# Summing four of seven pairs of modulation vectors by accumulating DMAs instead of matmuls with ones

## The chip, the cores and the metric

The kernel runs on one core of one Trainium2 chip. The metric is the time of the whole program on the device, in microseconds (us); the time before is 1242.71 us, the median of three runs (1241.77 to 1243.41). The engines are TensorE (PE; PEld is its weight load), VectorE (DVE), ScalarE (ACT), GpSimd (POOL) and SyncE (SP), which here only issues DMAs. Each runs its own instructions in a fixed order and waits on semaphores. POOL issues a few DMAs too, those that add to their destination among them.

## The reference

Two layers over 256 latent tokens of width 1024, with 256 context tokens beside them in the first layer. Each layer is a half-step feed-forward block, a mixer (neighbourhood attention in layer 0, a short convolution in layer 1) and a second feed-forward block. Each of these scales, shifts and gates its tokens by modulation vectors, which come from a conditioning vector through a large matrix:

```
for i in range(DEPTH):
    m = (s_c @ ada_w[i] + ada_b[i]).reshape(B, N_MOD, 1, D)     # 9 vectors of 1024 per layer
    mc = (s_cc @ ada_w[i] + ada_b[i]).reshape(N_MOD, D)         # the context's own
    x = half_step_ffn(x, m[:, 0], m[:, 1], m[:, 2], ...)        # shift, scale, gate
    ...
    hx = modulate(x, m[:, 3], m[:, 4])                          # mixer, gate m[:, 5]
    ...
    x = half_step_ffn(x, m[:, 6], m[:, 7], m[:, 8], ...)
```

`ada_w[i]` has 1024 x 9216 float32 entries, so the modulation vectors alone load some 75 MB. What follows is about how these vectors are summed.

## The kernel before, in words

All arithmetic is float32-like: a matrix is split into a high and a low part on ACT (high) and DVE (low), and a product takes three matmuls. PE's order is the program's. The other engines' instructions are placed by a scheduler that works with priorities, so their order can move when anything in the program moves; SP's DMAs too stand in one fixed order, and a DMA that waits holds back all that stand behind it.

The first feed-forward block runs on latent and context tokens together (`f0_mm`, the matmuls at L730, and `out_gemm`). Beside it, in the background, `stream` computes modulation vectors in seven groups of two; a "tick" after each few matmuls moves it on. For one group, `ada` loads 128 x 1024 blocks of `ada_w` (tile `ar`, L317), multiplies each by 128 values of the conditioning vector, one per partition, and adds it to an accumulator of 128 x 1024 on DVE (`acc`, L306 and L308). There are two buffers for accumulators. What is left is a sum over the 128 partitions: four matmuls with a tile of ones (L343), 512 columns each, which write to a PSUM bank; DVE adds the bias (L344), and two DMAs on SP put the vectors into a table in DRAM, `scr` (L346). Groups are counted from 0; groups 0 to 2 are the gates, shifts and scales that are needed first (vectors 2, 3 and 4 of layer 0 for both token sets), group 3 is vectors 5 and 6 of layer 0, group 4 is 7 and 8, groups 5 and 6 are vectors 0 to 3 of layer 1. Later vectors are made in another way on POOL (`sum_up`), with an add-accumulating DMA of 4 KB into `scr` (L358).

The vectors are read from `scr` as rows that are broadcast over partitions (`gate`, L378) or as columns (`mrow` at L394, in `fold_cols`).

Then comes attention. In each of 16 steps a pair of heads gets its scores (L1052 on PE); DVE adds a bias to them (L1056). A bias tile is loaded by SP with small DMAs from a table (L933) and gets a mask added on POOL (L937). There are four bias tiles, so the load of a bias waits until the scores two pairs earlier have been read. Between the steps the projections of keys, values and queries run as a filler, and at the end the output projection (`wo`).

Of the kernel before, what the change touches and what calls it, by code (L numbers as in the profile page):

```python
# [10 lines left out]
F32 = mybir.dt.float32  # L11
# [3 lines left out]
ALU = mybir.AluOpType  # L15
# [3 lines left out]
P = 128  # L19
D = 1024  # L20
# [39 lines left out]
ROPE_EARLY = 70  # L60
S_EARLY = 40
V_LAG = 1
AHEAD = 3
P_EARLY = 70
V_EARLY = 70
# [11 lines left out]
def backbone_kernel(  # L77
# [6 lines left out]
    nc = tc.nc  # L84
    sync = nc.sync
# [16 lines left out]
    def nm(s):  # L102
        uid[0] += 1
        return f"{s}_{uid[0]}"
# [10 lines left out]
    def tpb(s="tp"):  # L115
        return bank("tp", s)
# [125 lines left out]
    win_sb = cp.tile([P, 64], F32, tag="wmask", name="wmask")  # L242
# [4 lines left out]
    lnc = cp.tile([P, 2], F32, tag="lnc", name="lnc")  # L247
# [29 lines left out]
    scr = [tc.dram_tile([2, 9 * D], F32, name=f"scr{i}") for i in range(2)]  # L277
# [10 lines left out]
    def ada(vecs):  # L288


        acc = {}

        def accumulate(l, m, k, w):
            with ExitStack() as st:
                for i in gate_ins + (last_lo if on_pool[0] else []):
                    st.enter_context(tc.issue_after(i.ins))
                for i, vec in enumerate(vecs):
                    if vec[:2] != (l, m):
                        continue
                    if k == 0:  # L300
                        acc[i] = hp.tile([P, D], F32, tag="acc", bufs=2, name=nm("acc"))
                    sc = cst[:, k, vec[2]:vec[2] + 1]
                    for h in range(2):
                        src, a = (c[:, h * 512:(h + 1) * 512] for c in (w, acc[i]))
                        if k == 0:
                            nc.vector.tensor_scalar(a, src, sc, None, op0=ALU.mult)  # L306
                        else:
                            nc.vector.scalar_tensor_tensor(out=a, in0=src, scalar=sc, in1=a,  # L308
                                                           op0=ALU.mult, op1=ALU.add)
            if on_pool[0] and k == KC - 1:  # L310
                sums.extend((vec, acc[i]) for i, vec in enumerate(vecs) if vec[:2] == (l, m))

        loaded = []
        for l, m in dict.fromkeys((l, m) for l, m, _ in vecs):
            for k in range(KC):
                w = hp.tile([P, D], F32, tag="ar", bufs=3, name=nm("ar"))
                sync.dma_start(w, ada_w[l, k * P:(k + 1) * P, m * D:(m + 1) * D])  # L317
                loaded.append((l, m, k, w))
                if len(loaded) > (ADA_LAG if gate_ins else 0):
                    accumulate(*loaded.pop(0))  # L320
                yield 1
        while loaded:
            accumulate(*loaded.pop(0))
            if loaded:
                yield 1
        if on_pool[0]:
            return
        n = 2 * len(vecs)
        if not bias_rows:
            bias_rows.append(hp.tile([P, 512], F32, tag="adab", name=nm("adab")))  # L330
            nc.gpsimd.memset(bias_rows[0], 0.0)
        bt = bias_rows[0]
        for i, (l, m, v) in enumerate(vecs):
            sync.dma_start(bt[64 * i:64 * i + 64:32], ada_b[l, m * D:(m + 1) * D].rearrange("(a b) -> a b", b=512))
        yield 1
        yield 1
        yield 1
        rows = hp.tile([P, 512], F32, tag="adar", name=nm("adar"))
        ps = tpb("ada")
        for i in range(len(vecs)):  # L340
            for h in range(2):
                j = 2 * i + h
                nc.tensor.matmul(ps[32 * j:32 * j + 32, :], ones, acc[i][:, h * 512:(h + 1) * 512], start=True, stop=True)  # L343
        nc.vector.tensor_tensor(out=rows[:32 * n], in0=ps[:32 * n], in1=bt[:32 * n], op=ALU.add)  # L344
        for i, (l, m, v) in enumerate(vecs):
            sync.dma_start(scr[l][v, m * D:(m + 1) * D].rearrange("(a b) -> a b", b=512),  # L346
                           rows[64 * i:64 * i + 64:32, :])
        yield 1

    def sum_up():  # L350
        mark = [nc.gpsimd.tensor_tensor(out=warm, in0=g[0:1, 0:1], in1=lnc[0:1, 0:1], op=ALU.add)
# [10 lines left out]
    made = [0]  # L362
# [46 lines left out]
    def queued(ins):  # L409

        es = ExitStack()
        for i in ins:
            es.enter_context(tc.issue_after(i.ins))
        return es
# [17 lines left out]
    def finish_stats(st):  # L432
        mv = sm.tile([P, 2], F32, tag="mv", bufs=6, name=nm("mv"))
        norm_ins[:] = [nc.vector.bn_aggr(mv, st)]
        rs = sm.tile([P, 1], F32, tag="rs", bufs=6, name=nm("rs"))
        nc.gpsimd.tensor_tensor(out=rs, in0=mv[:, 1:2], in1=lnc[:, 0:1], op=ALU.add)
        nc.gpsimd.tensor_tensor(out=rs, in0=rs, in1=lnc[:, 1:2], op=ALU.pow)
        return mv, rs

    fence = []  # L440
    norm_ins = []
    first_mv = []

# [58 lines left out]
    def run(gen):  # L502
        for _ in gen:
            pass
# [247 lines left out]
    for q, (k0, n) in enumerate(steps):  # L752
        nxt = start_step(*steps[q + 1]) if q < 4 else iter(())
        for g in range(6 * n):
            for _ in range(NS[min(q, 2)][g]):
                next(nxt, 0)
            k = k0 + g // 6
            if k < KC - 1:
                z, part = ZP[g % 6]
                for j in range(3):  # L760
                    f0_part(b0[j][z], 0, u0, j, z, k, part)
            else:
                f0_mm(b0[g % 6 // 2][g % 2], 0, u0, g % 6 // 2, g % 2, (k,))
        run(nxt)
    sync.dma_start(win_sb, win_mask)
    sync.dma_start(rope, rope_tab.rearrange("(t p) a b -> p t a b", p=P))
    w_early[0] = W_EARLY
# [156 lines left out]
    def bias_pair(h, qt, last=False):  # L924


        for hh in (h, h + 1):
            if last:
                bt = rtile(256).rearrange("p (a b) -> p a b", a=4)
            else:  # L930
                bt = hp.tile([P, 4, 64], F32, tag="bias", bufs=4, name=nm("bias"))
            for i in range(2):
                bias_dma[:] = [sync.dma_start(bt[64 * i:64 * i + 64],  # L933
                                              bass.AP(na_rpb_rev.tensor,
                                                      na_rpb_rev.offset + hh * 465 + (7 - 2 * qt - i) * 31 - 48,
                                                      [[1, 64], [31, 4], [1, 64]]))]
            nc.gpsimd.tensor_tensor(out=bt, in0=bt, in1=win_sb[:, ::-1].unsqueeze(1).to_broadcast([P, 4, 64]),  # L937
                                    op=ALU.add)
            BIAS[hh, qt] = bt[:, :, ::-1]

    w_qkv = na_w_qkv[0]
# [94 lines left out]
        res.append(Late(2, rest))  # L1036

    oT = []
    bias_dma = []
    KV, Q = [], []  # L1040

    def scores(h, qt):
# [99 lines left out]
    fill_some(A_PRE + 1)  # L1142
    for i in range(len(steps) + LAG + V_LAG):
        if i == NX_AT:
            new_x(0, 0, s2t)
            for t in range(2):
                for h in range(2):
                    sync.dma_start(xscr[t * P:(t + 1) * P, h * 512:(h + 1) * 512], xt[t][h])
        while i + AHEAD < len(steps) and len(KV) <= steps[i + AHEAD][0] // 4:
            fill_some(1)  # L1150
        if i < len(steps) and i % 2 == 0:
            with tc.high_priority(offset=S_EARLY):
                prs[i], prs[i + 1] = scores(*steps[i])
            for j in range(i + 2 if i <= BIAS_AT else i + 4, i + (3 if i < BIAS_AT else 5), 2):
                if i % 2 == 0 and j < len(steps):
                    bias_pair(*steps[j], j > BIAS_AT + 2)
        credit += rate[min(i, len(rate) - 1)]
        n = int(credit)
        credit -= n
        if i >= V_LAST and fin is None:  # L1160
            run(fill)
            fin = last_filler()
            fill = islice(fin, 10)
        fill_some((n + 1) // 2)
        if i == len(steps) + LAG - 1:
            run(fill)
        if 0 <= i - LAG < len(steps):
            with tc.high_priority(offset=P_EARLY):
                probs_T(*steps[i - LAG], prs.pop(i - LAG))
        fill_some(n // 2)  # L1170
        j = i - LAG - V_LAG
        if j >= 0 and steps[j][1] == 1:
            with tc.high_priority(offset=V_EARLY):
                values(steps[j][0])
    run(fill)
    run(islice(fin, 1))

    def first_unit(u, *behind):
# [8 lines left out]
    phase = tc.tile_pool(name="ph2", bufs=1)  # L1187
    hp = phase.__enter__()
    on_pool[0] = True
    sync.dma_start(scr[1][0, 4 * D:9 * D].rearrange("(a b) -> a b", a=16), ada_b[1, 4 * D:9 * D].rearrange("(a b) -> a b", a=16))  # L1190
    ext[0] = 2

    v0 = made[0]
# [128 lines left out]
```

## Time and profile before

| | |
|---|---|
| median of three runs | 1242.71 us |
| the profiled execution | 1243.97 us, of it the span from first to last instruction 1242.2 us |
| PE busy | 1224.0 us, 99% of the span |
| DVE, ACT, POOL busy | 77%, 52%, 7% |
| chain that ended last | PE 89%, DVE 4%, DMA 2%, ACT 2% |
| first feed-forward block | until about 385 us |
| attention | about 385 to 595 us |

Busy times are shares of the span, and a busy PE is not PE at its peak. The chain that ended last is followed back from the last instruction, at each step to what released it. The view of stretches gives for each engine its busy time in a piece of the span with the number of its instructions, the granted clock of TensorE as a share of full speed, the busy share of the 16 DMA engines and what they moved.

### The profile page before, as it was taken

The numbers are of one execution on the slowest core, as the hardware profiler recorded it, in microseconds if no ns is written. First come the engines' busy times: TensorE is split into PE (matmuls) and PEld (weight loads), VectorE is DVE, ScalarE is ACT, GpSimd is POOL, SyncE is SP. The second block draws the span as 40 slices with busy tenths as digits, with TensorE's granted clock in tenths as the row PEclk, the third lists the DMA queues.
The fourth block names the chain that finished last, engine by engine and source line by source line (L and its number), as shares of the span: only waits on it lengthen the run. The fifth ranks groups of instructions, "written<-read, shape, count | busy, mean of one in ns | idle before, by whom it ended". The sixth has DMA issues, their size and how long they took to land.

```text
span 1242.2 us, 17397 instructions
## 1 busy us (share of the span) xinstructions
PE 1224.0 (99%) x5878; PEld 999.2 (80%) x5878; DVE 962.5 (77%) x1675; ACT 646.6 (52%) x1233; POOL 81.7 (7%) x93
## 2 busy tenths in 40 slices
PE   8999999999999999999999999999999999999997
PEld 5787778778778878887888888888888877888886
DVE  3598997778868767889877677878868798777646
ACT  2433132321325566678787635678635745677531
POOL 0000000000001111120000020020200100000100
PEclk9999999999999999999999999999999999999999
DMA  9976578778852654563899857899776664899741
GB/s 298 303 248 231 183 239 293 260 254 281 296 180 68 177 119 96 125 149 108 258 315 287 278 202 251 231 284 319 228 253 217 212 221 153 231 289 275 245 155 67
DMA packets 232241, 275.69 MB, mean 222 GB/s; under 512 B 59558, under 2 KB 178846, under 8 KB 232152
## 3 DMA queue, kind: packets, MB, share of 16 engines
q1 hardware_dynamic: 231956, 274.54, 71.9%
q8 instruction: 46, 0.75, 0.2%
q14 instruction: 43, 0.35, 0.1%
q0 software_dynamic: 160, 0.02, 0.0%
q10 hardware_dynamic: 36, 0.02, 0.0%
HBM read 265.27 MB, written 2.20 MB: 215 GB/s over the span
## 4 chain that ended last, share of the span: by engine, by line
PE 89%; DVE 4%; DMA 2%; ACT 2%; issue 1%; SPq 1%; POOL 0%; DVEq 0%; ACTq 0%
PE f L730 19%; PE w L171 17%; PE w L172 17%; PE w L174 17%; PE wkv L171 2%; PE wkv L172 2%; PE wkv L174 2%; PE wc L171 1%; PE wc L174 1%; PE wc L172 1%; DMA ar<-in_ada_w_dram 1%; PE S L1052 1%; PE hT L455 1%; PE PT L1077 1%; DVE wcl L220 1%
## 5 line engine op out<-in xcount | busy, mean ns | idle before, releaser
L220 DVE TENSOR_TENSOR w1l<-w1r,w1h 128x512 fp32r<-128x512 f32 (+1 forms) x352 | 226.9, 689 | 45.0 <-ACT w1h L217 44.0
L217 ACT ACTIVATE w1h<-w1r 128x512 fp32r<-128x512 f32 (+1 forms) x352 | 198.7, 618 | 116.8 <-DMA w1r<-in_ffn_w_in_dram 46.1
L171 PE MATMUL w<-w1h,hTh 128*128 128x512 f32 x528 | 206.3, 391 | 1.2 <-ACT hTh L119 1.2
L172 PE MATMUL w<-w1l,hTh 128*128 128x512 f32 x528 | 205.5, 389 | 0.0
L308 DVE SCALAR_TENSOR_TENSOR acc<-ar,cst,acc 128x512 f32<-128x512 f32 x266 | 189.3, 759 | 10.3 <-DMA ar<-in_ada_w_dram 10.2
L171 PE MATMUL w<-w2h,gh 128*128 128x512 f32 (+1 forms) x446 | 173.4, 389 | 0.0
L172 PE MATMUL w<-w2l,gh 128*128 128x512 f32 (+1 forms) x446 | 172.2, 387 | 0.0
L217 ACT ACTIVATE w2h<-w2r 128x512 fp32r<-128x512 f32 x176 | 101.5, 624 | 135.4 <-PE w L174 119.4
L220 DVE TENSOR_TENSOR w2l<-w2r,w2h 128x512 fp32r<-128x512 f32 x176 | 118.3, 713 | 59.1 <-ACT w2h L217 57.2
L174 PE MATMUL w<-w1h,hTl 128*128 128x512 f32 x528 | 162.6, 389 | 0.0
L174 PE MATMUL w<-w2h,gl 128*128 128x512 f32 (+1 forms) x446 | 136.1, 386 | 0.0
L730 PE MATMUL f<-h0h,w1h 128*128 128x512 f32 x352 | 132.4, 392 | 1.9 <-ACT w1h L217 1.5
L730 PE MATMUL f<-h0l,w1h 128*128 128x512 f32 x352 | 133.1, 391 | 0.0
L730 PE MATMUL f<-h0h,w1l 128*128 128x512 f32 x352 | 132.8, 390 | 0.0
L171 PEld LDWEIGHTS w<-w1h,hTh 128*128 128x128 f32 x528 | 99.1, 188 | 22.6 <-ACT hTh L119 2.1
L174 PEld LDWEIGHTS w<-w1h,hTl 128*128 128x128 f32 x528 | 99.0, 188 | 20.9 <-DVE hTl L120 0.4
L172 PEld LDWEIGHTS w<-w1l,hTh 128*128 128x128 f32 x528 | 99.2, 188 | 20.5 <-DVE w1l L220 0.2
L171 PEld LDWEIGHTS w<-w2h,gh 128*128 128x128 f32 x446 | 83.8, 188 | 19.2 <-issue 1.7
L172 PEld LDWEIGHTS w<-w2l,gh 128*128 128x128 f32 x446 | 83.8, 188 | 17.0 <-DVE w2l L220 0.5
L174 PEld LDWEIGHTS w<-w2h,gl 128*128 128x128 f32 x446 | 83.3, 188 | 17.1
L730 PEld LDWEIGHTS f<-h0h,w1h 128*128 128x128 f32 x352 | 65.7, 188 | 19.6 <-issue 3.4
L730 PEld LDWEIGHTS f<-h0l,w1h 128*128 128x128 f32 x352 | 65.6, 188 | 14.3 <-issue 0.8
(216 smaller groups left out, 1783.1 us busy)
## 6 DMA issues: line engine op xcount, KB each, us to landing
w1r<-in_ffn_w_in_dram SPq DMA_DIRECT2D x340, 256.0 KB
ar<-in_ada_w_dram SPq DMA_DIRECT2D x128, 512.0 KB
w2r<-in_ffn_w_out_dram SPq DMA_DIRECT2D x88, 512.0 KB
ar<-in_ada_w_dram SPq DMA_DIRECT2D x32, 256.0 KB
wcr<-in_sc_w_in_dram SPq DMA_DIRECT2D x32, 256.0 KB
wkvr<-in_na_w_qkv_dram SPq DMA_DIRECT2D x24, 256.0 KB
wqr<-in_na_w_qkv_dram SPq DMA_DIRECT2D x8, 512.0 KB
wor<-in_na_w_out_dram SPq DMA_DIRECT2D x8, 512.0 KB
```

The costliest lines, as they stand in the source:

```text
L171: nc.tensor.matmul(ps, lh, rh, start=first and i == 0, stop=False)
L172: nc.tensor.matmul(ps, lh, rl, start=False, stop=False)
L174: nc.tensor.matmul(ps, ll, rh, start=False, stop=last and i == n - 1)
L217: last_split[:] = [nc.scalar.activation(hi[:, a:a + m // W_HI], raw[:, a:a + m // W_HI], AF.Copy)]
L220: last_lo[:] = [nc.vector.tensor_tensor(out=lo[:, a:b], in0=raw[:, a:b], in1=hi[:, a:b].bitcast(F32), op=ALU.subtract)]
L308: nc.vector.scalar_tensor_tensor(out=a, in0=src, scalar=sc, in1=a, op0=ALU.mult, op1=ALU.add)
L455: nc.tensor.transpose(ps[:, k * P:(k + 1) * P], z[h][:, k * P:(k + 1) * P], ident)
L730: nc.tensor.matmul(ps, w, hT0[k][part == 1], start=(k == part == 0), stop=(k == KC - 1 and part == 1))
L1052: nc.tensor.matmul(banks[i], (qh, ql, qh)[f][ps, qs], (kh, kh, kl)[f][ps, :], start=f == 0, stop=f == 2)
L1077: nc.tensor.transpose(pt[:, k * P:(k + 1) * P], pr[:, k * P:(k + 1) * P], ident)
```

## The change

Groups 3 to 6 no longer use matmuls for the sum over partitions. Their accumulators are stored to DRAM, 128 rows of 2048 numbers for the two vectors of a group, and POOL issues DMAs that add the lower half of the rows to the upper half, seven times, until one row is left; two more add that row to `scr`. Since these last ones add, `scr` has to hold the bias first: two copies in DRAM put it there early, which replace one such copy of fewer vectors later. The tree of group 3 is issued at once; those of groups 4, 5 and 6 are kept, and one level of each is issued behind each pair of bias additions in attention. A drain of POOL is added at the start of the second feed-forward block.

```
+BY_TREE = (3, 4, 5, 6)
+TREE_LATE = (4, 5, 6)
+TREE_GAP = 3
...
+        if made[0] in BY_TREE:
+            yield 1
+            yield 1
+            T = tc.dram_tile([P, 2 * D + 64], F32, name=nm("accd"))
+            for i in range(len(vecs)):
+                sync.dma_start(T[:, i * D:(i + 1) * D], acc[i])
+            levels = tree(T, vecs)
+            if made[0] in TREE_LATE:
+                late_trees.append(levels)
+            else:
+                run_all(levels)
+            for _ in range(TREE_GAP):
+                yield 1
+            return
...
+    def tree(T, vecs):
+        n = P // 2
+        while n:
+            nc.gpsimd.dma_start(T[0:n, 0:2 * D], T[n:2 * n, 0:2 * D], accum_op=ALU.add)
+            n //= 2
+            yield
+        for i, (l, m, v) in enumerate(vecs):
+            nc.gpsimd.dma_start(scr[l][v:v + 1, m * D:(m + 1) * D], T[0:1, i * D:(i + 1) * D], accum_op=ALU.add)
+            yield
...
+    def late_levels(n):
+        for _ in range(n):
+            while late_trees:
+                levels = late_trees.pop(0)
+                if next(levels, 0) is None:
+                    late_trees.append(levels)
+                    break
...
+    for l, v, r in ((0, 0, slice(5 * D, 9 * D)), (1, 0, slice(0, 9 * D))):
+        sync.dma_start(scr[l][v, r].rearrange("(a b) -> a b", a=16), ada_b[l, r].rearrange("(a b) -> a b", a=16))
     sync.dma_start(win_sb, win_mask)
...
                 if i % 2 == 0 and j < len(steps):
                     bias_pair(*steps[j], j > BIAS_AT + 2)
+            with queued(bias_add):
+                late_levels(3)
...
 on_pool[0] = True
-    sync.dma_start(scr[1][0, 4 * D:9 * D].rearrange("(a b) -> a b", a=16), ada_b[1, 4 * D:9 * D].rearrange("(a b) -> a b", a=16))
+    with queued(rs_ins):
+        nc.gpsimd.drain()
```

On PE, at the end of group 3 in the first feed-forward block, this stood before (`f` is a PSUM bank of the block's matmuls, `h0` and `w1` their operands, `h` and `l` at a name's end the high and low part):

```order
L730 MATMUL f_323_1971<-h0h_571,w1h_1892 128x512
L730 MATMUL f_323_1971<-h0h_571,w1l_1893 128x512
L730 MATMUL f_323_1971<-h0l_572,w1h_1892 128x512
L343 MATMUL ada_1997<-acc_1630,ones 32x512 x2
L343 MATMUL ada_1997<-acc_1795,ones 32x512 x2
L730 MATMUL f_326_2005<-h0h_180,w1h_1865 128x512
```

and this stands there now, with the lines of the changed kernel:

```order
L771 MATMUL f_323_1971<-h0h_549,w1l_1895 128x512
L771 MATMUL f_323_1971<-h0l_550,w1h_1894 128x512
L771 MATMUL f_323_1971<-h0h_571,w1h_1894 128x512
L771 MATMUL f_323_1971<-h0h_571,w1l_1895 128x512
L771 MATMUL f_323_1971<-h0l_572,w1h_1894 128x512
L771 MATMUL f_325_2008<-h0h_180,w1h_1867 128x512
```

The two rows of matmuls with ones are gone, here and at three more places; all other rows of PE keep their order.

On POOL, near the start of the steps of attention, this stood before (`bias` is a bias tile, `wmask` the mask):

```order
L937 TENSOR_TENSOR bias_3928<-bias_3928,wmask 128x256
L937 TENSOR_TENSOR bias_3932<-bias_3932,wmask 128x256
L937 TENSOR_TENSOR bias_4021<-bias_4021,wmask 128x256
L937 TENSOR_TENSOR bias_4025<-bias_4025,wmask 128x256
L937 TENSOR_TENSOR bias_4114<-bias_4114,wmask 128x256
L937 TENSOR_TENSOR bias_4118<-bias_4118,wmask 128x256
```

and this stands there now (`accd` is a tree's table in DRAM, and the rows by columns are those of one level):

```order
L980 TENSOR_TENSOR bias_3911<-bias_3911,wmask 128x256
L370 DMA accd_2379<-accd_2379 64x2048
L370 DMA accd_2756<-accd_2756 64x2048
L370 DMA accd_3188<-accd_3188 64x2048
L980 TENSOR_TENSOR bias_4003<-bias_4003,wmask 128x256
L980 TENSOR_TENSOR bias_4007<-bias_4007,wmask 128x256
L370 DMA accd_2379<-accd_2379 32x2048
L370 DMA accd_2756<-accd_2756 32x2048
L370 DMA accd_3188<-accd_3188 32x2048
L980 TENSOR_TENSOR bias_4099<-bias_4099,wmask 128x256
L980 TENSOR_TENSOR bias_4103<-bias_4103,wmask 128x256
```

Behind each pair of additions stand three DMAs, one level of each late tree; it goes on so for nine pairs.

On SP, late in attention, this stood before (`wor` are weights of the output projection; the names in brackets are what a row waits for, `DMAHW` being an earlier DMA of SP and `DMASW` one of POOL):

```order
L212 DMA wor_5479<-in_na_w_out_dram 128x2x512 [waits DMAHW2_49,DVE_49,Activation_49]
L212 DMA wor_5592<-in_na_w_out_dram 128x2x512 [waits DMAHW3_49,DVE_49,Activation_49]
L933 DMA bias_5020<-in_na_rpb_dram 64x4x64 [waits DMAHW4_49,DVE_49]
L933 DMA bias_5020<-in_na_rpb_dram 64x4x64 [waits DMAHW5_49]
L933 DMA bias_5024<-in_na_rpb_dram 64x4x64 [waits DMAHW6_49,DVE_49]
```

and this stands there now:

```order
L976 DMA bias_4923<-in_na_rpb_dram 64x4x64 [waits DMAHW0_49]
L435 DMA mrow_87<-scr_119 8x128 [waits DMAHW1_49,DMASW7_49]
L215 DMA wor_5485<-in_na_w_out_dram 128x2x512 [waits DMAHW2_49,DVE_49,Activation_49]
L215 DMA wor_5598<-in_na_w_out_dram 128x2x512 [waits DMAHW3_49,DVE_49,Activation_49]
L435 DMA mrow_87<-scr_119 8x128 [waits DMAHW4_49,DMASW2_49]
L976 DMA bias_5026<-in_na_rpb_dram 64x4x64 [waits DMAHW5_49,DVE_49]
```

Two loads of modulation columns for layer 1 (`mrow`), which stood at the end of the first feed-forward block, now stand between the loads of weights and biases, and each waits for a DMA of POOL: the first for the first add of group 5 into `scr`, the second for the second one, which POOL issues behind the next pair of bias additions.

## Rows read from the trace of the kernel before

**Rows 1.** Stretches of the span, busy time by engine; the header names the columns.

```profile
core 0: us, PE busy (x) PEld busy (x) DVE busy (x) ACT busy (x) POOL busy (x), PEclk, DMA share, GB/s
200.00:250.00 50.00, 50.00 (x225) 40.47 (x224) 38.48 (x62) 17.85 (x31) 0.00 (x0) 1.00 0.82 280
...
300.00:350.00 50.00, 50.00 (x225) 40.47 (x224) 42.75 (x69) 14.41 (x25) 0.00 (x0) 1.00 0.86 288
425.00:435.00 10.00, 10.00 (x50) 8.39 (x49) 9.96 (x20) 6.55 (x14) 0.00 (x0) 1.00 0.56 203
500.00:550.00 50.00, 49.22 (x372) 43.93 (x371) 41.17 (x93) 36.21 (x80) 10.67 (x14) 1.00 0.59 116
650.00:700.00 50.00, 50.00 (x223) 41.39 (x222) 36.41 (x62) 36.56 (x65) 0.00 (x0) 1.00 0.99 292
```

**Rows 2.** What PE waited for: total us, times, longest us.

```profile
PE f L730 <- ACT w1h L217: 1.5, 2, 0.8
```

**Rows 3.** Timeline of PE at group 3: start us, us, instruction.

```profile
221.03 0.39 PE L730 MATMUL f<-h0h,w1l 128*128 128x512 f32 x1
221.25 0.39 PE L730 MATMUL f<-h0l,w1h 128*128 128x512 f32 x1
221.57 1.06 PE L343 MATMUL ada<-acc,ones 128*32 128x512 f32 x8
...
222.91 0.39 PE L730 MATMUL f<-h0h,w1l 128*128 128x512 f32 x1
```

**Rows 4.** The same at group 6, first and last row around the matmuls.

```profile
360.94 0.39 PE L730 MATMUL f<-h0l,w1h 128*128 128x512 f32 x1
...
362.59 0.39 PE L172 MATMUL w<-w2l,gh 128*128 128x512 f32 x1
```

**Rows 5.** Waits of all engines from 200 to 300 us.

```profile
ACT w2h L217 <- PE w L174: 14.7, 1, 14.7
```

**Rows 6.** Timeline of POOL; in brackets idle time before, and its end.

```profile
385.80 0.19 POOL L436 TENSOR_TENSOR rs<-mv,lnc 128x1 f32<-128x1 f32 x1 [381.64 <-DVE mv L434]
...
424.20 0.74 POOL L937 TENSOR_TENSOR bias<-bias,wmask 128x256 f32<-128x256 f32 x1 [3.86 <-DMA bias<-in_na_rpb_dram]
...
447.04 0.74 POOL L937 TENSOR_TENSOR bias<-bias,wmask 128x256 f32<-128x256 f32 x1 [1.00 <-DMA bias<-in_na_rpb_dram]
451.75 0.73 POOL L937 TENSOR_TENSOR bias<-bias,wmask 128x256 f32<-128x256 f32 x1 [3.97 <-DMA bias<-in_na_rpb_dram]
...
519.99 0.83 POOL L937 TENSOR_TENSOR bias<-bias,wmask 128x256 f32<-128x256 f32 x1 [1.56 <-DVE wol L220]
...
529.78 0.86 POOL L937 TENSOR_TENSOR bias<-bias,wmask 128x256 f32<-128x256 f32 x1 [0.34 <-DMA bias<-in_na_rpb_dram]
```

**Rows 7.** Timeline of DVE, score additions in attention.

```profile
454.31 0.75 DVE L1056 TENSOR_TENSOR S<-S,bias 128x256 f32<-128x256 f32 x2
...
469.32 0.82 DVE L1056 TENSOR_TENSOR S<-S,bias 128x256 f32<-128x256 f32 x2
...
536.02 0.75 DVE L1056 TENSOR_TENSOR S<-S,bias 128x256 f32<-128x256 f32 x2
```

**Rows 8.** The accumulating DMA at L358: issue on POOL in ns, landing.

```profile
L358 POOL DMA_DIRECT2D scr<-red x5: 997/997/1118, 725.1 to 1154.1; - x5
...
DMA to landing us min/median/max: 2.6/3.4/4.0
```

**Rows 9.** Timeline of SP's DMA issues in attention.

```profile
432.78 3.30 SPq L212 DMA_DIRECT2D wkvr<-in_na_w_qkv_dram  x6
...
515.55 4.77 SPq L212 DMA_DIRECT2D wor<-in_na_w_out_dram  x2
522.72 2.63 SPq L933 DMA_DIRECT2D bias<-in_na_rpb_dram  x4
```

**Rows 10.** Timeline of ACT, splits of weights in attention.

```profile
458.12 0.63 ACT L217 ACTIVATE wkvh<-wkvr 128x512 fp32r<-128x512 f32 x1
...
549.96 2.19 ACT L217 ACTIVATE woh<-wor 128x512 fp32r<-128x512 f32 x4
```

More of the change, by code (lines that the diff above doesn't have):

```diff
@@ L348, in ada, with run_all @@
         yield 1
+    def tree(T, vecs):
[7 more added lines that the diff above has]
+            yield
+    def run_all(levels):
+        for _ in levels:
+            pass
+    def late_levels(n):
[5 more added lines that the diff above has]
+                    break
+    late_trees = []
     def sum_up():
@@ L436, in finish_stats @@
         nc.gpsimd.tensor_tensor(out=rs, in0=mv[:, 1:2], in1=lnc[:, 0:1], op=ALU.add)
-        nc.gpsimd.tensor_tensor(out=rs, in0=rs, in1=lnc[:, 1:2], op=ALU.pow)
+        rs_ins[:] = [nc.gpsimd.tensor_tensor(out=rs, in0=rs, in1=lnc[:, 1:2], op=ALU.pow)]
         return mv, rs
-    fence = []
+    fence, rs_ins = [], []
     norm_ins = []
@@ L936, in bias_pair @@
                                                       [[1, 64], [31, 4], [1, 64]]))]
-            nc.gpsimd.tensor_tensor(out=bt, in0=bt, in1=win_sb[:, ::-1].unsqueeze(1).to_broadcast([P, 4, 64]),
-                                    op=ALU.add)
+            bias_add[:] = [nc.gpsimd.tensor_tensor(out=bt, in0=bt, in1=win_sb[:, ::-1].unsqueeze(1).to_broadcast([P, 4, 64]),
+                                    op=ALU.add)]
             BIAS[hh, qt] = bt[:, :, ::-1]
@@ L1038, in backbone_kernel @@
     oT = []
-    bias_dma = []
+    bias_dma, bias_add = [], []
     KV, Q = [], []
@@ L1175, in backbone_kernel @@
     run(fill)
+    assert not late_trees
     run(islice(fin, 1))
```

## The prediction

> **What bounds the kernel now.** I read the table of stretches first [rows 1]. Between 200 and 350 us, in the first feed-forward block, TensorE is busy for all of every stretch, with 225 matmuls in 50 us, at a granted clock of 1.00; the DMA engines are busy 0.82 to 0.86 of the time. From 500 to 550 us, late in attention, PE has 0.8 us of gaps. Then the list of what PE waited for [rows 2]: its longest entry inside the work is 1.5 us in the whole run. So in the block where the change takes instructions off PE, the end of the block is set by the sum of PE's own instructions, and a microsecond taken from PE there is a microsecond of the end, unless something else becomes late. Then the timeline of PE around the instructions that go [rows 3, 4], and last, for what is added, the timelines of GpSimd (POOL), VectorE (DVE) and SyncE (SP) in attention [rows 6, 7, 9].
>
> **What goes.** A group of two modulation vectors ended with four matmuls against a tile of ones, which the trace records as 8 passes, one row of 1.06 us [rows 3]; with seven groups that is 56 passes. Their times overlap with the neighbours', so the price is read from the neighbours' starts. Neighbouring matmuls start 0.22 us apart (221.03 to 221.25; 50 us over 225 of them is 0.222 too). From the start of the last matmul ahead, 221.25, to the second one behind, 222.91, are 1.66 us; without the eight passes two steps, 0.45 us, would stand there. That is 1.21 us for the group at 221 us. For the group at 361 us it is 362.59 - 360.94 - 0.45 = 1.20 us [rows 4]; the two between them have the same pattern. Four groups go: 4 x 1.20 = 4.8 us off PE. The order of PE shows that nothing else on PE moved: the rows ahead of and behind the gap are the same. With the matmuls go four DVE additions, eight loads of 4 KB and eight stores of 4 KB; PE is the bound there, so I count these as nothing.
>
> **What comes, in the feed-forward block.** Eight stores of an accumulator, 128 x 1024 x 4 bytes = 512 KB each, on SP's queue, and the tree of group 3 on POOL. At the 280 GB/s of [rows 1] a store is 1.9 us of DMA work, 15 us in all over about 180 us, so the DMA share rises from 0.82 to 0.86 to about 0.90 to 0.95. The bound from below is nothing: at a share of 0.99 between 650 and 700 us PE still has all 50.00 us [rows 1]. The bound from above is that each store delays a weight load just when PE has none left, 8 x 1.9 = 15 us. I take the value near the lower end, because weights run ahead: ScalarE stood 14.7 us at a stretch waiting for PE to free a weight buffer [rows 5], and a store of 1.9 us fits into that. SP's wait for the last multiply-add ahead of the second store takes the place of a wait of the same kind ahead of the old store of sums. The accumulator of the next group waits for a store of the buffer it reuses, but the first vector's store stands in SP's order before the second vector is finished, so it has a long lead. The DVE order of this block is reshuffled by a few places; I allow 0.4 us for splits that come late through it (ends 0 and 1.5 us, the upper one being what PE waited for splits in the whole run, rows 2). Group 3's tree is nine DMAs on a POOL that has nothing else to do before the first normalization; even at 10 us each they are done 90 us after the group at 221 us, and that normalization is at 385.8 [rows 6].
>
> **What comes, in attention.** Three trees are issued level by level, three DMAs behind each pair of bias additions on POOL. No accumulating DMA of this size is in the trace. The nearest is the 4 KB one at L358 [rows 8]: 1.0 us to issue, 2.6 to 4.0 us to land (I take 3.4). So a step adds about 3 us of issuing to POOL, between additions of 0.74 us.
> - *First level.* It follows the addition that ends at 424.9 us and has until 447.8, when the next pair of additions ends [rows 6]. From below it takes 2.6 us to land; from above, 3 x 3 x 512 KB = 4.7 MB (reading the source, reading and writing the destination) at the 203 GB/s of that stretch [rows 1], 23 us, just the time there is. An overrun of 5 us would move the additions of 451.8 to 457, and their scores are at 469.3 [rows 6, 7]. The weights that SP asks for at 432.8 us [rows 9] are split at 458 us [rows 10], 25 us later. I count nothing.
> - *Later levels* have half the bytes each, and the next issue is one pair, about 10 us, later. Nothing.
> - *The last adds into the parameter rows* matter most, because SP waits for them. SP's order now has two loads of such rows (L435) that wait for POOL's DMAs. The first holds back only loads of output weights (515.55 before the change, rows 9), whose splits start at 549.96 [rows 10]: 30 us of cover. The second waits for the add issued second behind the pair of additions that ends at 520.8 [rows 6]: 1.0 us for the DMA ahead, then 3.4 us to land, 525.2. Queued behind it are the bias loads that SP issued at 522.72 [rows 9], so they go 2.9 us late with the issue of the load itself. Their second addition ended at 530.6 [rows 6]; it ends at 533.5 now, and the scores that read it are at 536.0 [rows 7]. There was 5.4 us of cover and 2.5 us is left: nothing on the path. If that cover were gone, each further microsecond would be one of DVE, and of the end. SP's later loads catch up, since their own waits are for scores.
> - POOL's drain after the normalizations stands where POOL has no work for over 100 us; the two 16- and 36-KB copies of the bias rows are issued while PE already has its weights. Nothing.
>
> **The sum.** The profiled execution took 1243.97 us (span 1242.2 and 1.77 around it): 1243.97 - 4.8 + 0.4 = 1239.6. The median of the runs shown is 1.3 us below the profiled one, so I predict 1238.3 us for the median, 0.36% less than 1242.71.
>
> **Rivals.**
> 1. *The gain is given back.* Late bias loads in attention, or stores in the feed-forward block, eat most of 4.8 us. For it: PE has gaps from 500 us on already, and cover of 2.5 us is thin. Against it: SP and POOL move earlier together with everything else. By the working above the scores wait once the add lands later than 3.4 + 2.5 = 5.9 us after its issue; at 10 us they wait 4.1 us, and the time is 1238.3 + 4.1 = 1242.4. As much would come from two or three stores that each hold a weight load by 1.9 us.
> 2. *POOL becomes the bound of attention: slower.* Scores at 454.3 and 536.0 [rows 7] are eight pairs apart, 10.2 us a pair. POOL has two additions and three DMAs in a pair: 2 x 0.74 + 3t. It decides from t = 2.9 us. At t = 4 us a pair takes 13.5 us, 3.3 us too long, eight times 26 us, of which the head start of the additions (469.3 - 451.8 = 17.5 us) hides two thirds; some 9 us remain: about 1247 us. For it: the DMAs have up to 64 rows of 8 KB where the traced one has 16 pieces of 256 bytes. Against it: the rows halve at each level, the long first level has 20 us to itself, and the five traced issues took 0.997 to 1.118 us [rows 8].
>    The Trainium skill (SBUF — State Buffer, "SBUF: two separate sides") speaks for this rival: GpSimd writes the descriptors of its DMAs itself and is shut out while VectorE runs some kinds of operation, so that such a DMA took about 3100 ns where 620 ns were normal. At 3.1 us, an estimate from that page, a pair would take 10.8 us and eight pairs 5 us too long, all of it inside the head start. The trace shows no such issue so far (rows 8).
> 3. *The time PE loses is not on the path.* PE would only idle elsewhere: 1242.7. Against it are the full stretches of [rows 1] on both sides of every group. That the change does not remove the matmuls is excluded by the order.
>
> **How the numbers follow.** Forecast 0.67, given back (rivals 1 and 3) 0.23, slower 0.10. The forecast's own range is 1237.0 (4.8 us in full, and 0.9 us for DVE's additions and runs that fall low) to 1240.2. Within 0.2%, 2.5 us, which is about what a measurement of this kernel can tell from no change, lie 1240.2 to 1245.2: rivals 1 and 3. The range for 8 in 10 leaves out rival 2 and the upper end of rival 1: 1236.8 to 1243.0. Chances: faster 0.67, same 0.23, slower 0.10.
>
> **What would show it.** In the profile after: ones-matmuls in 24 passes instead of 56; 225 matmuls still in each 50 us between 200 and 350, and the first normalization on POOL about 4.5 us before 385.8 us [rows 6]; the new DMAs of POOL at 1 to 1.5 us each; a wait of SP for a POOL DMA of 2 to 4 us near 517 to 521 us; no wait of DVE's score additions for POOL. Wrong it would be if PE shows waits for split weights or VectorE in the feed-forward block, or if DVE waits for bias additions at 530 us and later, or if the end comes earlier by much more than the first normalization does.

## The result and the profile after

The changed kernel takes 1249.1 us (median of 6 runs, 1245.43 to 1250.82) beside 1242.44 for the kernel before (6 runs, 1241.12 to 1243.41): a ratio of 1.005, 95% interval 1.0034 to 1.0066. I had forecast 1238.3. It is slower by about 6.7 us where 0.36% less was expected. The profiled execution took 1248.97 us, span 1247.2.

The stretches of the kernel after, with the columns of [rows 1] (the four of 2 us follow the second wait told of below):

```profile
200.00:250.00 50.00, 48.51 (x213) 39.50 (x212) 37.42 (x59) 15.78 (x29) 5.07 (x6) 1.00 0.93 304
250.00:300.00 50.00, 46.10 (x190) 36.89 (x189) 38.21 (x61) 9.86 (x17) 2.34 (x3) 0.93 0.88 298
300.00:350.00 50.00, 48.09 (x211) 39.18 (x210) 38.08 (x62) 14.82 (x27) 0.00 (x0) 1.00 0.87 290
500.00:550.00 50.00, 49.28 (x361) 43.85 (x359) 43.12 (x91) 36.95 (x79) 17.75 (x22) 1.00 0.56 114
...
258.00:260.00 2.00, 1.40 (x4) 0.58 (x2) 2.00 (x5) 0.50 (x1) 1.38 (x2) 0.50 0.77 240
260.00:262.00 2.00, 1.82 (x4) 1.46 (x5) 2.00 (x5) 0.13 (x1) 0.18 (x1) 0.50 0.84 256
262.00:264.00 2.00, 2.00 (x6) 1.58 (x5) 1.20 (x2) 0.00 (x0) 0.00 (x0) 0.50 0.90 336
264.00:266.00 2.00, 2.00 (x9) 1.62 (x9) 0.51 (x2) 0.00 (x0) 0.00 (x0) 0.94 1.03 395
```

TensorE no longer fills the stretches of the first feed-forward block. What it waited for from 200 to 360 us (total us, times, longest), where the kernel before had nothing:

```profile
PE f L771 <- DVE w1l L223: 3.7, 4, 2.0
PE w L175 <- DVE w2l L223: 3.1, 1, 3.1
PE w L174 <- ACT gh L122: 0.8, 1, 0.8
```

So the low halves of split weights came late from VectorE. Its timeline ahead of the first wait (TensorE stood from 229.5 to 230.8 us), with idle time in brackets:

```profile
222.27 0.74 DVE L311 SCALAR_TENSOR_TENSOR acc<-ar,cst,acc 128x512 f32<-128x512 f32 x1
225.68 1.41 DVE L311 SCALAR_TENSOR_TENSOR acc<-ar,cst,acc 128x512 f32<-128x512 f32 x2 [2.66 <-DMA ar<-in_ada_w_dram]
228.74 1.41 DVE L311 SCALAR_TENSOR_TENSOR acc<-ar,cst,acc 128x512 f32<-128x512 f32 x2 [1.65 <-DMA ar<-in_ada_w_dram]
230.07 1.28 DVE L223 TENSOR_TENSOR w1l<-w1r,w1h 128x512 fp32r<-128x512 f32 x2
231.27 0.74 DVE L311 SCALAR_TENSOR_TENSOR acc<-ar,cst,acc 128x512 f32<-128x512 f32 x1
231.94 1.28 DVE L223 TENSOR_TENSOR w1l<-w1r,w1h 128x512 fp32r<-128x512 f32 x2
```

and ScalarE's, which makes the high halves that these splits read:

```profile
222.57 1.15 ACT L220 ACTIVATE w1h<-w1r 128x512 fp32r<-128x512 f32 x2 [0.81 <-PE f L771]
223.94 1.15 ACT L220 ACTIVATE w1h<-w1r 128x512 fp32r<-128x512 f32 x2 [0.21 <-ACT w1h L220]
```

The first two splits had their inputs from 223.7 us on and the other two from 225.1, while VectorE was idle for 2.66 us up to 225.68 and for 1.65 us up to 228.74. It did not do them, since multiply-adds of the modulation stream stood ahead of them and waited for their weight rows (`ar`). (The Trainium skill, PSUM — Partial Sum Buffer, "Engine vs sequencer instructions", says that VectorE's queue is strictly first in, first out; these rows agree: splits ready at 223.7 us started at 230.07.) At the same place the kernel before had the splits at 225.25 and 227.13, 4.8 us earlier, with fewer multiply-adds between:

```profile
222.67 0.49 DVE L306 TENSOR_SCALAR acc<-ar,cst 128x512 f32<-128x512 f32 x1 [4.15 <-PE ada L343]
...
224.07 0.75 DVE L308 SCALAR_TENSOR_TENSOR acc<-ar,cst,acc 128x512 f32<-128x512 f32 x1
225.25 1.29 DVE L220 TENSOR_TENSOR w1l<-w1r,w1h 128x512 fp32r<-128x512 f32 x2 [0.44 <-ACT w1h L217]
226.47 0.75 DVE L308 SCALAR_TENSOR_TENSOR acc<-ar,cst,acc 128x512 f32<-128x512 f32 x1
227.13 1.29 DVE L220 TENSOR_TENSOR w1l<-w1r,w1h 128x512 fp32r<-128x512 f32 x2
```

There the group's first multiply waited 4.15 us for the ones-matmuls of the group ahead, which free its accumulator, and that held the stream back. In the changed kernel this multiply starts 5 us earlier and waits for its load alone:

```profile
217.70 0.88 DVE L309 TENSOR_SCALAR acc<-ar,cst 128x512 f32<-128x512 f32 x2 [1.11 <-DMA ar<-in_ada_w_dram]
```

VectorE's idle time for `ar` from 200 to 360 us, before (L306, L308):

```profile
DVE acc L308 <- DMA ar<-in_ada_w_dram: 8.2, 13, 1.3
...
DVE acc L306 <- DMA ar<-in_ada_w_dram: 2.0, 2, 1.0
```

and after:

```profile
DVE acc L311 <- DMA ar<-in_ada_w_dram: 22.3, 17, 2.7
DVE acc L309 <- DMA ar<-in_ada_w_dram: 10.9, 5, 3.9
```

Ahead of the second wait VectorE shows the same picture, with five splits behind multiply-adds; ScalarE had made the high halves of four of them by 249.0 us:

```profile
254.44 1.41 DVE L311 SCALAR_TENSOR_TENSOR acc<-ar,cst,acc 128x512 f32<-128x512 f32 x2 [1.93 <-DMA ar<-in_ada_w_dram]
255.78 3.09 DVE L223 TENSOR_TENSOR w2l<-w2r,w2h 128x512 fp32r<-128x512 f32 x5
```

This wait is dearer than its length. TensorE's timeline:

```profile
253.01 0.39 PE L174 MATMUL w<-w2h,gh 128*128 128x512 f32 x1
256.51 0.50 PE L175 MATMUL w<-w2l,gh 128*128 128x512 f32 x1 [3.11 <-DVE w2l L223]
...
262.48 0.63 PE L175 MATMUL w<-w2l,gh 128*128 128x512 f32 x1
262.90 0.63 PE L174 MATMUL w<-w2h,gh 128*128 128x512 f32 x1
...
264.45 0.40 PE L174 MATMUL w<-w2h,gh 128*128 128x512 f32 x1
264.68 0.39 PE L175 MATMUL w<-w2l,gh 128*128 128x512 f32 x1
```

After the 3.11 us of standing the matmuls start 0.42 to 0.43 us apart instead of 0.23, and the stretches from 258 to 264 us show a granted clock of 0.50, the 1.2 GHz level. From 253.01 to 264.45 are 11.44 us for 18 steps of 0.225, 4.05 us: 7.4 us lost, of them 3.9 in two waits (3.11 us, and 0.8 for `gh`) and 3.5 in slower steps, most of them at that clock. Counted in the same way, the waits at 229 and 348 us cost 2.1 and 2.8 us. In all 12.3; less the 4.8 us of the removed matmuls that is 7.5. The first normalization on POOL is 7.17 us later than the 385.80 of [rows 6]:

```profile
392.97 0.19 POOL L477 TENSOR_TENSOR rs<-mv,lnc 128x1 f32<-128x1 f32 x1 [132.79 <-DVE mv L475]
...
409.39 0.52 POOL L477 TENSOR_TENSOR rs<-mv,lnc 128x1 f32<-128x1 f32 x1 [6.04 <-DVE mv L475]
...
591.33 0.19 POOL L477 TENSOR_TENSOR rs<-mv,lnc 128x1 f32<-128x1 f32 x1 [29.06 <-DVE mv L475]
```

The last of the four of this block is at 409.39 and the next at 591.33: attention takes 181.94 us. Before:

```profile
402.24 0.53 POOL L436 TENSOR_TENSOR rs<-mv,lnc 128x1 f32<-128x1 f32 x1 [6.04 <-DVE mv L434]
...
584.80 0.19 POOL L436 TENSOR_TENSOR rs<-mv,lnc 128x1 f32<-128x1 f32 x1 [30.16 <-DVE mv L434]
```

182.56 us. All of the loss is in the first feed-forward block: 7.15 us up to its fourth normalization, 0.6 less in attention and 1.5 less behind it (655.9 us to the end of the span, 657.4 before; why is open) make the 5.0 us between the two profiled executions. Below, the place of its fourth normalization (402.24 before, 409.39 after) is the measure of the block in one profiled execution. It holds a difference that has nothing to do with the block: TensorE's matmul 1001 by the count of the trace, the same one in every run and ahead of the first sum that goes, starts anywhere from 199.64 to 201.63 us. In the kernel before and in the run narrow_no_tree it is

```profile
200.40 0.39 PE L730 MATMUL f<-h0h,w1h 128*128 128x512 f32 x1
201.63 0.39 PE L767 MATMUL f<-h0h,w1h 128*128 128x512 f32 x1
```

So the table also gives the time from that matmul to the fourth normalization, which is the better measure; it is 201.84 us in the kernel before, and 7.67 us more after the change, beside the 7.5 counted above.

### The profile page after: what moved, and what is told of

The parts are those of the page before. It is cut to its first block, busy times and chain, and to the rows that moved or that the text cites. A ratio compares the mean times of both kernels' runs of the same rounds, so it can differ in the third digit from the quotient of the medians.

```text
span 1247.2 us, 17355 instructions
## 1 busy us (share of the span) xinstructions
PE 1222.8 (98%) x5846; PEld 1000.7 (80%) x5846; DVE 957.8 (77%) x1671; ACT 644.2 (52%) x1233; POOL 111.9 (9%) x129
## 4 chain that ended last, share of the span: by engine, by line
PE 75%; DVE 10%; DMA 9%; ACT 2%; issue 2%; SPq 1%; POOL 0%; DVEq 0%; ACTq 0%
PE w L174 16%; PE w L175 15%; PE w L177 15%; PE f L771 9%; DMA ar<-in_ada_w_dram 7%; DVE acc L311 3%; DVE w1l L223 3%; PE wkv L174 2%; PE wkv L175 2%; PE wkv L177 2%; PE wc L174 2%; PE wc L177 2%; PE wc L175 2%; DMA w1r<-in_ffn_w_in_dram 1%; PE S L1095 1%
## 5 line engine op out<-in xcount | busy, mean ns | idle before, releaser
L223 DVE TENSOR_TENSOR w1l<-w1r,w1h 128x512 fp32r<-128x512 f32 (+1 forms) x352 | 230.8, 699 | 40.8 <-ACT w1h L220 38.0
L223 DVE TENSOR_TENSOR w2l<-w2r,w2h 128x512 fp32r<-128x512 f32 x176 | 113.4, 686 | 57.9 <-ACT w2h L220 56.7
L771 PEld LDWEIGHTS f<-h0h,w1l 128*128 128x128 f32 x352 | 65.9, 188 | 19.3 <-DVE w1l L223 5.8
```

The lines of the kernel that those rows point to most:

```text
L223: last_lo[:] = [nc.vector.tensor_tensor(out=lo[:, a:b], in0=raw[:, a:b], in1=hi[:, a:b].bitcast(F32), op=ALU.subtract)]
L771: nc.tensor.matmul(ps, w, hT0[k][part == 1], start=(k == part == 0), stop=(k == KC - 1 and part == 1))
```

## The experiments

Theory A: the order. Multiply-adds stand ahead of splits, and the loads' lateness is handed on to TensorE. Theory B: the traffic of the 512 KB stores makes the loads late. Theory C: group 3's tree (216 to 260 us) does.

| run | stores | tree in the block | VectorE's order | fourth normalization | from matmul 1001 to it | median, us | ratio to before, 95% interval |
|---|---|---|---|---|---|---|---|
| after | full | yes | new | 409.39 | 209.51 | 1249.1 | 1.0050 (1.0034 to 1.0066) |
| after_again | full | yes | new | 406.36 | 206.47 | 1248.36 | 1.0042 (1.0028 to 1.0056) |
| no_tree | full | no | new | 406.03 | 205.74 | 1245.43 | 1.0034 (1.0019 to 1.0049) |
| no_tree_again | full | no | new | 407.88 | 207.43 | 1245.9 | 1.0033 (1.0020 to 1.0045) |
| narrow_no_tree | 1/32 | no | like the new | 405.99 | 204.35 | 1246.31 | 1.0033 (1.0020 to 1.0046) |
| narrow | 1/32 | 1/32 | like the new | 406.12 | 205.15 | 1256.44 | 1.0110 (1.0093 to 1.0126) |
| stores_added | full | no | like the old | 403.12 | 201.84 | 1242.02 | 0.9995 (0.9987 to 1.0004) |
| tree_added | full | yes | like the old | 403.24 | 202.18 | 1242.45 | 0.9997 (0.9989 to 1.0006) |
| before_behind | none | no | old, behind splits | 401.83 | 201.84 | 1242.83 | 1.0002 (0.9994 to 1.0011) |
| behind_splits | full | yes | new, behind splits | 399.91 | 199.77 | 1239.46 | 0.9981 (0.9973 to 0.9990) |
| tree_after_4 | full | yes | as behind_splits | 398.55 | 198.67 | 1240.63 | 0.9982 (0.9973 to 0.9991) |
| tree_after_5 | full | yes | as behind_splits | 398.20 | 198.56 | 1239.6 | 0.9973 (0.9962 to 0.9984) |
| behind_all_late | full | no, later | as behind_splits | 398.28 | 198.26 | 1241.84 | 0.9992 (0.9984 to 1.0001) |

**Without the trees.**

```diff
-            levels = tree(T, vecs)
-            if made[0] in TREE_LATE:
-                late_trees.append(levels)
-            else:
-                run_all(levels)
```

> The changed kernel without any of its trees: the eight stores of accumulators stay, no accumulating DMA is issued, so the vectors of groups 3 to 6 are missing from the sums. VectorE's order of instructions is the same as in the changed kernel, row for row. Theory A (order: accumulates of the next group stand ahead of the weight splits on VectorE, and wait for their loads there): 1247 to 1250 us, the two waits of TensorE for weights near 230 and 253 us stay. Theory B (traffic of the stores delays the loads): 1246 to 1249 us. Theory C (group 3's tree, which runs from 216 to 260 us, delays the loads): 1240 to 1243 us, the waits at 230 and 253 us gone.

1245.43 us, just below what B expected and between A and C. The wait at 230 us is gone, those at 252 (2.6 us) and 346 us (0.9) stay. The one at 230 us says little, since it is 0.4 us in after_again, which is the changed kernel itself. C alone falls, and A's range was missed too.

**Narrow transfers.**

```diff
+TW = 32
-                sync.dma_start(T[:, i * D:(i + 1) * D], acc[i])
+                sync.dma_start(T[:, i * TW:(i + 1) * TW], acc[i][:, 0:TW])
...
-            nc.gpsimd.dma_start(T[0:n, 0:2 * D], T[n:2 * n, 0:2 * D], accum_op=ALU.add)
+            nc.gpsimd.dma_start(T[0:n, 0:2 * TW], T[n:2 * n, 0:2 * TW], accum_op=ALU.add)
...
```

> The changed kernel with 32 of the 1024 columns of each accumulator stored and summed (the other columns of groups 3 to 6 are left out of the sums): the same number of DMAs, a thirtieth of the bytes, so hardly any traffic. VectorE still has up to 10 accumulates ahead of the splits of one panel. Theory A (order): 1246 to 1250 us. Theory B (traffic of stores) and theory C (tree): 1236 to 1240 us, which is the before less the 4.8 us of the removed matmuls. If both order and traffic are needed: 1240 to 1245 us.

1256.44 us, slower than any theory expected, by two things. The first block takes 3.3 us more than before, with hardly any traffic. The rest is in attention, and of another kind. SP's waits in narrow from 500 to 550 us, then its VectorE and TensorE:

```profile
SPq L436 <- DMA scr<-accd: 19.7, 2, 11.6
```

```profile
544.94 0.43 DVE L1100 TENSOR_TENSOR S<-S,bias 128x256 f32<-128x256 f32 x1 [5.05 <-POOL bias L981]
```

```profile
547.30 1.11 PE L1121 MATMUL PT<-ident,pr 128*128 128x128 f32 x4 [5.27 <-DVE kTl L124]
```

SP's load of a parameter row waited 11.6 us for a tree's last add, the bias loads queued behind it came late, and so the scores. That is the mechanism of my rival 1. The add itself was not slow (the eight of this run landed 2.0 to 5.7 us after their issue) but was issued late, at 531 us, behind bias additions at 528.25 and 530.28; the first of these had itself waited 10.83 us for its bias load, so SP and POOL held each other up in turn. Why it comes to that in this kernel I did not follow further. In the changed kernel the same wait is harmless:

```profile
SPq L435 <- DMA scr<-accd: 5.7, 2, 3.3
```

**Narrow transfers without trees** (both edits above).

> The run narrow without its trees: only 16 KB stores of 32 columns of each accumulator are left of the change, no accumulating DMA (the vectors of groups 3 to 6 are missing from the sums). VectorE's order is that of narrow, with up to 10 accumulates ahead of the splits of one panel. Theory A (the order alone is enough): the fourth rs of the first block stands 3 to 5 us later than the kernel before has it (402.2), as in narrow, and the time is 1244 to 1248 us, for what narrow lost in attention (loads of mrow that wait on SP for the trees' last adds, with the bias loads behind them) goes with the trees. Theory B and C (traffic or POOL's DMAs are needed for the loss): 1236 to 1240 us, rs at 397 to 399.

1246.31 us, the block's end 3.75 us late, of which 1.23 stand at matmul 1001 already. So the block takes 2.5 us more than before, and the 4.8 us of the removed matmuls are lost as well, although what is added are eight stores of 16 KB. VectorE's idle time for `ar` from 200 to 360 us is 27.2 us here (10.2 before): without the traffic too, the loads are late for a stream that runs ahead. TensorE's waits there from 200 to 360 us:

```profile
PE f L767 <- DVE w1l L224: 2.7, 2, 2.2
PE w L175 <- ACT gh L123: 1.9, 1, 1.9
```

The order alone is enough: B and C fall as necessary causes.

**The stores added to the kernel before.**

```diff
+        if made[0] in (3, 4, 5, 6):
+            T = tc.dram_tile([P, 2 * D + 64], F32, name=nm("accd"))
+            for i in range(len(vecs)):
+                sync.dma_start(T[:, i * D:(i + 1) * D], acc[i])
```

> The kernel before, with the eight 512 KB stores of the accumulators of groups 3 to 6 added (to a DRAM tile that nothing reads) and the matmuls against ones kept: nearly VectorE's order of the kernel before, with the traffic of the stores. Theory A (order): 1242 to 1244 us, as the kernel before. Theory B (traffic): 1246 to 1254 us (the loss of 12 us less what the order would take). Theory C (tree): 1242 to 1243 us.

1242.02 us. The DMA engines are about as busy as in the changed kernel (there 0.93, 0.88 and 0.87 in these stretches), TensorE waits for nothing, and the block takes the 201.84 us that it takes in the kernel before:

```profile
200.00:250.00 50.00, 50.00 (x225) 40.49 (x224) 38.91 (x63) 17.16 (x30) 0.00 (x0) 1.00 0.88 297
250.00:300.00 50.00, 50.00 (x225) 40.48 (x224) 42.33 (x69) 11.85 (x21) 0.00 (x0) 1.00 0.87 296
300.00:350.00 50.00, 50.00 (x225) 40.48 (x224) 41.27 (x66) 14.30 (x25) 0.00 (x0) 1.00 0.90 293
```

**Multiply-adds behind splits.** The rule that the kernel has from its second phase on, for the groups after group 3 too:

```diff
-                for i in gate_ins + (last_lo if on_pool[0] else []):
+                for i in gate_ins + (last_lo if on_pool[0] or made[0] > BY_TREE[0] else []):
```

> The changed kernel, with the accumulates of the groups after group 3 told to stand on VectorE behind the latest weight split in program order (as the kernel does already from the second phase on); stores and trees unchanged. Theory A (order): 1236 to 1241 us, the gain of the removed matmuls is seen. Theory B and C (traffic, tree): 1246 to 1250 us, as the changed kernel.

1239.46 us: stores and trees as in the changed kernel, the loss gone and a gain there. At the place shown above its VectorE does all four splits as soon as ScalarE has made their halves, 6.6 us earlier:

```profile
223.49 2.66 DVE L223 TENSOR_TENSOR w1l<-w1r,w1h 128x512 fp32r<-128x512 f32 x4 [1.48 <-ACT w1h L220]
226.06 1.41 DVE L311 SCALAR_TENSOR_TENSOR acc<-ar,cst,acc 128x512 f32<-128x512 f32 x2
```

Of the 4.8 us the block keeps 2.1 in this execution (199.77). TensorE still waits near 253 us, now for a product that stands behind multiply-adds on VectorE, which the rule does not move:

```profile
PE w L174 <- ACT gh L122: 1.7, 1, 1.7
PE w L177 <- DVE gl L123: 0.3, 1, 0.3
```

**The rule in the kernel before.** `last_lo if on_pool[0] or made[0] > 3`.

> The kernel before with the same rule as behind_splits: accumulates of the groups after group 3 stand behind the latest split; sums by matmuls against ones as before. Theory A: 1241.5 to 1243 us, as the kernel before, which has no wait of TensorE there to lose, so that the gain of behind_splits is the removed matmuls. Rival (the rule is a gain by itself, whatever sums the groups): 1238 to 1240 us.

1242.83 us: the rule by itself gives nothing. The gain of behind_splits is that of the removed matmuls.

**All trees late.** In behind_splits, `TREE_LATE = (3, 4, 5, 6)`.

> The run behind_splits with group 3's tree issued in attention as well, behind the same bias adds as the other three (nothing left out of the sums). VectorE's order is that of behind_splits. Theory A alone: as behind_splits, 1238.5 to 1240.5 us. Theory A with a part of C (the tree makes loads late, and the order hands the lateness on): 1236.5 to 1239 us, the wait of 1.7 us at 253 us smaller or gone. Against it: 9 more issues on POOL in attention (some 7 us of POOL) that delay bias adds: 1240 to 1245 us.

1241.84 us. The block takes 3.6 us less than before, in this execution three quarters of the 4.8. But attention takes 184.33 us where behind_splits took 182.33 (one profile each), and SP waits up to 5.0 us for a tree's last add there, 3.5 in behind_splits. So the condition named as against it came true; that the fourth tree's nine issues on POOL are what costs the 2 us is likely but not shown.

**The tree after another group.** In behind_splits the generator of group 3's tree is kept, and run after group 4's store, or group 5's.

> The run behind_splits with group 3's tree issued after group 4's store instead of after its own (nothing left out): VectorE's order is that of behind_splits, the tree no longer runs before 253 us. Theory A with a part of C (the tree makes loads late where it runs, and the order hands it on): the wait of 1.7 us for gh at 253 us is gone (0.3 us or less, as in behind_all_late), attention is as in behind_splits, so 1237 to 1239 us, unless the tree meets a wait of its own in the panels from 270 to 310 us (then 1239 to 1240.5 us). Theory A alone: 1239 to 1240 us.

> As tree_after_4, with group 3's tree issued after group 5's store, about 310 to 355 us. Theory A with a part of C: 1237 to 1239 us, unless the tree's late levels stand on POOL ahead of the rs additions at the end of the block (384 us; then 1240 to 1245 us). Theory A alone: 1239 to 1240 us.

The edit did not do what the expectations say. The tree's first DMA stands on POOL at 215.69 and 215.79 us, as in behind_splits (216.58), and the orders of VectorE and POOL are those of behind_splits, row for row: written later, it is placed where its data is ready. The two runs tell nothing on the tree. They are repeats of behind_splits: 0.9981, 0.9982 and 0.9973. That version beats both kernels.

**What the tree costs.** Two runs more, and a tree into a DRAM tile that nothing reads, in stores_added:

```diff
+            n = P // 2
+            while made[0] == 3 and n:
+                nc.gpsimd.dma_start(T[0:n, 0:2 * D], T[n:2 * n, 0:2 * D], accum_op=ALU.add)
+                n //= 2
```

> The run stores_added with group 3's tree added, seven accumulating DMAs on POOL into the DRAM tile that nothing reads, right behind its stores; sums by matmuls against ones as in the kernel before. VectorE's order is that of stores_added, row for row. The order alone decides (theory A): 1241.5 to 1243 us, no waits of TensorE from 200 to 360 us. The tree costs by itself (theory C): 1244 to 1247 us. Theory A with a part of C (it costs only where the order hands lateness on): 1242 to 1243.5 us.

> The changed kernel once more, beside no_tree_again on one chip, to tell whether the tree of group 3 costs anything under the changed kernel's order. Theory A alone: the two have the same time, 1245 to 1249 us. Theory A with a part of C: this one is 2 to 4 us above no_tree_again.

> The run no_tree once more, beside after_again (no sums of groups 3 to 6). Theory A alone: the time of after_again. Theory A with a part of C: 1244.5 to 1246.5 us, and 2 to 4 us below after_again.

With the old order, stores and tree together cost nothing that the times can tell (0.9997), and 0.34 us of the block in the profile. With the new one the medians are 3.7 and 2.5 us apart, as a part of C would have it, but the intervals overlap, and in the profiled executions of the second pair the block with the tree was the shorter (206.47 to 207.43; in the first pair 209.51 to 205.74). Whether the tree adds to what the order loses stays open.

## Why the prediction was wrong

- *The price of what goes* held as far as it can be seen: 12.3 us of waits and slow steps less 4.8 make 7.5, and 7.67 were measured; with the order mended the block takes 2.1 to 3.6 us less than before (four profiles), and with the 0.6 to 2.0 us that TensorE still waits there this is 4.1 to 4.4 of the 4.8.
- *The eight stores* were rightly put near the lower end of 0 to 15 us: stores_added and tree_added are not slower than the kernel before.
- *The step that failed* is "The DVE order of this block is reshuffled by a few places; I allow 0.4 us for splits that come late through it (ends 0 and 1.5 us". The late splits and products cost 12.3 us in the profiled execution. By the time from matmul 1001, with the 4.8 us that went, the six profiles with the new order or one like it lost 7.3 to 12.5 us; 7.3 is narrow_no_tree (2.5 + 4.8), which has next to nothing else of the change. What the sum called a term of 0.4 us is therefore larger than the whole gain. The bound was misread: the 1.5 us of [rows 2] are two waits at 11.39 and 28.09 us, long before group 3, for high halves, which ScalarE makes (`ACT w1h`). TensorE's list of waits in the kernel before has none for VectorE's low halves. It was also wrong in kind: waits seen in an order in which splits stood ahead are no bound for another order. I had shown that TensorE's order was the same but for the removed rows, and took VectorE's for harmless by the number of rows moved. What counts is which instruction with a late input now stands ahead of one that TensorE needs.
- *"Weights run ahead"*, from ScalarE's 14.7 us of waiting [rows 5], held for the high halves ahead of the first wait here (223.7 us), but not for all loads: ScalarE waited 12.5 us in all for output weights (`w2r`) from 200 to 360 us, at most 5.1 (3.3 and 2.9 before). The low halves are made by another engine, and its queue was the late one.
- *The accumulator's reuse* was looked at only as a wait that could be added. It was also a wait that went: the ones-matmuls' hold on the next group's first multiply (4.15 us at 222.67) had kept the stream behind, and with it gone group 4 starts 5 us earlier. That removing it is what led to the new order is argued from the rows; shown is that the order, however it came about, makes the loss, and that moving the multiply-adds behind the splits mends it.
- *Attention* held, though landings were misjudged: POOL's issues took 0.76 to 1.37 us (forecast 1 to 1.5), the tree's own landed in 3.0 to 13.1 us and the last adds in 2.1 to 6.7 (forecast 3.4), SP waited 3.3 us at the longest (forecast 2 to 4), and no score waited for a bias. The rows of the tree's DMAs, issue in ns (least, median, most), and landing:

```profile
L370 POOL DMA_DIRECT2D accd<-accd x28: 755/806/1372, 215.9 to 506.6; - x28
...
DMA to landing us min/median/max: 3.0/5.4/13.1
```

  Rival 2 needed 2.9 us an issue, and did not occur; the time of about 3100 ns that the Trainium skill (SBUF — State Buffer, "SBUF: two separate sides") gives for a GpSimd that is shut out is in none of the 28 rows. Rival 1's mechanism is real but did not decide here.
- *The sign of the worst case*: I gave slower 0.10, for a mechanism in attention. The block in which TensorE was full, and so had no slack on any of its inputs, should have had the larger part of it. The prediction did name what would show it wrong, waits of PE for split weights in the feed-forward block, and that is what the profile shows.

## What to carry to other kernels

Where an engine is full, look at the order of every engine that feeds it: an instruction that waits for a DMA, ahead of one that the full engine needs, turns lateness of that DMA into lateness of the end. A buffer's release is also a brake; before taking away the instruction that releases it late, ask what will run earlier and where it will queue. If the change is worth its traffic, pin the filler behind the critical work explicitly: here one line turned 0.5% slower into 0.2% faster.

## What was not expected of the hardware

- Stands of 3.11 and 0.8 us cost TensorE nearly as much again: 3.5 us in slower steps, most of them at the 1.2 GHz level, from 257 to 264 us. At the same place 1.7 us of standing in behind_splits left the granted clock at 1.00, and 1.86 us in narrow_no_tree were followed by 0.50 from 258 to 260 us. Near 350 us a stand of 1.98 us in the changed kernel and one of 2.20 us in narrow_no_tree left it at 1.00, and one of 1.99 us in no_tree_again was followed by 0.56 from 348 to 350 us; what decides between the two these runs do not tell.
- An accumulating DMA from DRAM to DRAM took 0.76 to 1.37 us to issue, with 64 rows of 8 KB as with one, and 3.0 to 13.1 us to land; 4 MB more of stores at a DMA share of 0.87 to 0.90 did not slow TensorE at all while the order was right (stores_added), and a tree with them cost the block 0.34 us at 0.89 to 0.93 (tree_added).
